# Own raw buffers and an earlier load for the modulation blocks of merge and out projection, and the neighbourhood scores in one matmul

## Chip, cores and metric

The kernel runs on one core of a Trainium2 chip. The metric is the device time of one execution in microseconds (us). TensorE (PE in the profile) multiplies, VectorE (DVE), ScalarE (ACT) and GpSimd (POOL) do elementwise work and reductions, and SyncE (SP) issues all of the loads. A DMA that SP cannot issue yet, because its buffer is still in use, holds every DMA behind it in SP's queue.

## What is computed

Two layers of a diffusion trunk. Each layer has two attention branches side by side, a gated merge of them, an output projection and a feed-forward network; 512 latent tokens and 256 context tokens go through the same weights. Cut to what matters here:

```python
for l in range(2):
    mod, mod_c = silu(c) @ w_mod[l] + b_mod[l], silu(c_ctx) @ w_mod[l] + b_mod[l]   # six vectors of 1024 each
    h, hc = modulated rms_norm of x (512 tokens) and of ctx (256 tokens), with sh1, sc1
    na_q, na_k, na_v, gq, gk, gv, ga, gb = split(h @ w_in[l]);  the same for hc
    s_win = einsum(q, k in its window) * SCALE + bias        # neighbourhood attention: 8 heads of 64
    s_ctx = einsum(q, k_ctx) * SCALE
    p = softmax(concatenate([s_win, s_ctx]))
    ya = p_win @ v_win + p_ctx @ v_ctx
    yb = grouped-query attention over all 768 keys (8 query heads, 2 key heads, rms norm and rotary)
    merged = sigmoid(ga) * (ya @ w_pa) + sigmoid(gb) * (yb @ w_pb)
    x = x + g1 * (merged @ w_o)                              # the same for ctx in layer 0
    h2 = modulated rms_norm of x, with sh2, sc2
    x = x + g2 * (silu(h2 @ w_a) * (h2 @ w_u)) @ w_ffn_out   # the same for ctx in layer 0
return rms_norm(x, final_norm)
```

`mod` is the modulation: for each token kind (latent, context) 48 blocks of 128 numbers in a layer. Blocks 0 to 15 are the shift and scale ahead of attention, 16 to 23 the gate g1, 24 to 39 the shift and scale ahead of the feed-forward network, 40 to 47 the gate g2.

## The kernel before

**Layout and arithmetic.** Activations lie feature by token: eight tiles of 128 features by 768 tokens. Every float32 product is made as three fp32r products (`steps`, L647): high part by high part, high by low, low by high. So each weight block is loaded raw into a buffer with the tag `wr` (`raw`, L626), ScalarE makes its high part `wh` (L640) and VectorE or, in most of layer 0, GpSimd makes its low part `wl` (L642). The pool of weights holds four raw buffers, three `wh` and three `wl`.

**Stages.** A layer runs through attention (`mixing`), `merge`, `out_proj` and `ffn`. In the trace layer 0's merge and output projection lie at about 430 to 620 us, layer 1's at about 1444 to 1560 us.

**Merge** (L1816). Two branches of eight steps each: the first (grouped-query branch) multiplies by `w_pb`, the second (neighbourhood branch) by `w_pa`. A step takes its gate (already there, or projected in this step by eight k-blocks of three matmuls for each of the token spans), loads and splits one weight block of 512 columns, runs the modulation blocks that `MODS` gives it, and then multiplies (`pp`) and joins on VectorE (L1866 to L1871).

**Output projection** (L1891). It runs over the tokens in two halves; in each half eight steps of 24 matmuls (`po`), with the residual added by VectorE (L1876). In the first half a step also loads and splits one block of `wo` and, where `MODS` says so, runs one modulation block.

**The modulation blocks.** `mod_one` (L727) loads one block of `wmodT`, 128 by 1024 float32 and 512 KB, into a raw buffer of the weights' pool and then reduces it on VectorE against the condition row (L722), once for each token kind: tiles `junk` (context) and `wr` (latent, in place) in the profile. `MODS` (L71) places 26 blocks (16 to 41) in layer 0, namely 7 in the first branch, 12 in the second (up to two in a step) and 7 in the output projection, and 8 blocks (40 to 47, latent only) in the second branch of layer 1. Load and reduction of a block stand next to each other in the program. The remaining blocks go beside the feed-forward network through another function, `two`.

**Order.** In merge and output projection the order on each engine, SP's queue included, is chosen by a scheduler that simulates the program with its own costs. In layer 0's attention only TensorE's order is written out. In layer 1's attention a planner (`Plan`, L309) books each instruction at a modelled cost and writes out the order of all five engines; a matmul costs it 13.3 ns and 0.4167 ns a column, at least 109 ns.

**Neighbourhood scores** (`na_pair`, L1424). A head's 512 queries go in four blocks of 128. Each block has 256 keys of its window and the 256 context keys. For each of the two halves of q (`qh`, `ql`) blocks 0 to 2 take two matmuls of 256 columns; block 3, whose window wraps around, takes three (128, 128 and 256 columns), with the keys at 384 ahead of those at 0. All of a block's matmuls of one half of q share their weights, and each is issued with a weight load of its own. The bias table `rpb` has three kinds of 256 columns, the third of them for block 3. `turn` (L1456) transposes the softmax into the key order that the values need.

Of the kernel before, what the change touches and what calls it, by code (L numbers as in the profile page):

```python
# [3 lines left out]

# [599 lines left out]
class Trunk:  # L604
# [122 lines left out]
    def mod_one(self, l, n, crow, junk):  # L727
        w = self.raw(self.d["wmodT"][l * 48 + n])
        for part in self.mod_parts(l, n, crow, junk):
            part(w)  # L730

# [692 lines left out]
    def na_pair(self, head, q, k, val, bias, out, i, pool, done=None):  # L1424
# [4 lines left out]
        def scores(s, b):  # L1429
            if b < 3:  # L1430
                parts = [(0, 256, P * b)]
            else:
                parts = [(0, P, P * b), (P, 256, 0)]
            parts.append((256, 512, S))
            for hl in range(2):
                for j, (lo, up, src) in enumerate(parts):
                    nc.tensor.matmul(
                        s[:, lo:up], q[hl][:, b * P : (b + 1) * P], k[:, src : src + up - lo],
                        start=(hl == 0 and j == 0), stop=(hl == 1 and j == len(parts) - 1), skip_group_check=True)
# [16 lines left out]
        def turn(c):  # L1456
            tp = self.ps("t", "tp")
            for b in range(2):
                for j in range(2):
                    to = 2 * j + b if c else 2 * b + j  # L1460
                    nc.tensor.transpose(
                        tp[:, to * P : (to + 1) * P], zs[b][:, (2 * c + j) * P : (2 * c + j + 1) * P], self.ident)
# [353 lines left out]
    def merge(self, l, h, ya, yd, gates, ahead, spans, pool, beside):  # L1816
# [20 lines left out]
        for br, (gname, y) in enumerate((("gb", yb), ("ga", ya))):  # L1837
# [3 lines left out]
            for j in range(KB):  # L1841
# [11 lines left out]
                if beside:  # L1853
                    for _ in range(MODS[l][br][j]):
                        beside.pop(0)()
# [35 lines left out]
    def out_proj(self, l, merged, x, nh, pool, beside):  # L1891
# [5 lines left out]
        for half in range(2):  # L1897
            a, b = half * nh, half * nh + nh
            acc = None
            for j in range(KB)[:: 1 - 2 * half]:  # L1900
# [4 lines left out]
                if half == 0 and beside and MODS[l][2][j]:  # L1905
                    beside.pop(0)()
# [385 lines left out]
    def run(self):  # L2292
# [3 lines left out]
        with (  # L2296
# [24 lines left out]
            for l in range(DEPTH):  # L2321
# [7 lines left out]
                with (  # L2329
# [12 lines left out]
                    def one(of, n):  # L2342
                        def run():
                            conditions()
                            self.mod_one(of, n, *rows)
                        return run

                    first = 40 if last else 16
                    ahead = first + sum(sum(m) for m in MODS[l])
                    beside = [one(l, n) for n in range(first, ahead)]  # L2350
                    with tc.tile_pool(name=f"m{l}", bufs=1, reuse_waits="tile") as pool_:
                        pool = _Bufs(pool_, dict(rs=2, qt=5), slots)
# [69 lines left out]
def kinds(a, b):  # L2422

    return [(f, u, s) for f, u, s in ((a, min(b, S), 0), (max(a, S), b, 1)) if f < u]

# [54 lines left out]
class Hidden:  # L2480
# [23 lines left out]
    def c21(self, ps):  # L2504
        self.t.nc.vector.tensor_tensor(self.lo, self.lo, ps, op=ALU.mult)
        return [*enumerate(self.parts(self.f), 1)]

# [78 lines left out]
def _layout(a):  # L2586
# [42 lines left out]
    d["rpb"] = np.where(inside, a["na_rpb"][:, :, dr, dc][:, :, :, None], np.float32(-BIG)).reshape(DEPTH, 8, P, 768)  # L2629
# [15 lines left out]
```

## Time and profile before

| | |
|---|---|
| median of 3 runs | 1946.68 us (1945.83 to 1948.26) |
| profiled execution | 1943.38 us, of which the span of its trace is 1940.7 us |
| TensorE busy | 1909.2 us of the span, 12300 matmuls, mean granted clock 0.998 |
| VectorE busy | 1471.7 us (76%) |
| ScalarE, GpSimd busy | 937.8 us (48%), 227.5 us (12%) |
| DMA | 210.85 MB, mean 109 GB/s |

The span runs from the first to the last instruction. A busy time is the time in which an engine has an instruction in work; matmuls overlap in part, so the pitch from one start to the next tells more of them than their own duration. "Idle before" is the time that an engine stood still ahead of an instruction, with what ended the wait behind an arrow. The granted clock is the share of TensorE's full clock that the throttle allowed.

### The profile page before, as it was taken

The numbers are of one execution on the slowest core, as the hardware profiler recorded it, in microseconds if no ns is written. First come the engines' busy times: TensorE is split into PE (matmuls) and PEld (weight loads), VectorE is DVE, ScalarE is ACT, GpSimd is POOL, SyncE is SP. The second block draws the span as 40 slices with busy tenths as digits, with TensorE's granted clock in tenths as the row PEclk, the third lists the DMA queues.
The fourth block names the chain that finished last, engine by engine and source line by source line (L and its number), as shares of the span: only waits on it lengthen the run. The fifth ranks groups of instructions, "written<-read, shape, count | busy, mean of one in ns | idle before, by whom it ended". The sixth has DMA issues, their size and how long they took to land.

```text
span 1940.7 us, 31522 instructions
## 1 busy us (share of the span) xinstructions
PE 1909.2 (98%) x12300; PEld 1764.5 (91%) x12300; DVE 1471.7 (76%) x2797; ACT 937.8 (48%) x1820; POOL 227.5 (12%) x132
## 2 busy tenths in 40 slices
PE   8999999999999999999999999999999999999998
PEld 6989999898889999999999888889988999999998
DVE  6468887769777888787868578898557587877785
ACT  4456666642226533343424345666553355544553
POOL 0432212214300000000000012132210000000000
PEclk9999999999999999999999999999999999999999
DMA  8121112235462134334443411022145532332332
GB/s 328 46 69 42 53 58 63 77 120 179 158 217 87 66 109 130 109 120 131 139 144 131 152 55 33 34 79 82 55 128 175 199 109 77 98 120 90 104 96 83
DMA packets 71670, 210.85 MB, mean 109 GB/s; under 512 B 8545, under 2 KB 10721, under 8 KB 71521
## 3 DMA queue, kind: packets, MB, share of 16 engines
q1 hardware_dynamic: 71520, 208.84, 32.9%
q8 instruction: 96, 1.57, 0.3%
q14 instruction: 54, 0.43, 0.1%
HBM read 196.75 MB, written 6.82 MB: 105 GB/s over the span
## 4 chain that ended last, share of the span: by engine, by line
PE 64%; DVE 5%; issue 1%; ACT 1%; DMA 1%; POOL 0%; SPq 0%; DVEq 0%; POOLq 0%; ACTq 0%
PE po L655 21%; PE qu L2021 14%; PE qv L2021 7%; PE pj L540 4%; PE qc L2021 3%; PE pj L655 3%; PE pf L655 3%; PE pp L655 2%; PE sc L540 2%; PE y L540 2%; PE tp L540 1%; PE pv L540 1%; ACT p L540 1%; DVE m L540 1%; DVE ptl L540 0%
## 5 line engine op out<-in xcount | busy, mean ns | idle before, releaser
L2021 PE MATMUL qu<-r,w 128*128 128x384 f32 (+1 forms) x1872 | 295.9, 310 | 0.3
L2021 PEld LDWEIGHTS qu<-r,w 128*128 128x128 f32 x1872 | 281.0, 189 | 5.0 <-DVE tt L2501 3.8
L1884 ACT ACTIVATE w<-wr 128x512 fp32r<-128x512 f32 x234 | 145.5, 625 | 107.6 <-DVE wr L2465 36.2
L655 PE MATMUL po<-ph,wh 128*128 128x512 f32 (+1 forms) x576 | 197.4, 343 | 0.0
L655 PE MATMUL po<-ph,wl 128*128 128x512 f32 (+1 forms) x576 | 196.8, 342 | 0.0
L655 PE MATMUL po<-pl,wh 128*128 128x512 f32 (+1 forms) x576 | 196.2, 341 | 0.0
L655 PE MATMUL pj<-h,wh 128*128 128x512 f32 (+1 forms) x512 | 182.1, 356 | 1.4 <-DVE ql L1256 1.1
L655 PE MATMUL pj<-h,wl 128*128 128x512 f32 (+1 forms) x512 | 176.8, 345 | 0.9 <-POOL wl L642 0.9
L655 PE MATMUL pj<-hl,wh 128*128 128x512 f32 (+1 forms) x512 | 176.6, 345 | 0.0
L1876 DVE SCALAR_TENSOR_TENSOR x<-po,G,x 128x256 f32<-128x256 f32 (+3 forms) x168 | 99.2, 596 | 100.7 <-PE po L655 99.7
L1888 DVE TENSOR_TENSOR w<-wr,w 128x512 fp32r<-128x512 f32 x234 | 159.3, 685 | 11.3 <-ACT w L1884 10.3
L640 ACT ACTIVATE wh<-wr 128x1024 fp32r<-128x1024 f32 (+1 forms) x109 | 101.3, 933 | 137.2 <-PE po L655 30.4
L2021 PE MATMUL qv<-r,w 128*128 128x384 f32 (+1 forms) x936 | 150.6, 309 | 0.3 <-ACT tt L2027 0.3
L2021 PEld LDWEIGHTS qv<-r,w 128*128 128x128 f32 x936 | 141.2, 190 | 0.5 <-ACT tt L2027 0.5
L782 POOL TENSOR_TENSOR rs<-rs,expo 128x2 f32<-128x2 f32 (+2 forms) x7 | 5.5, 784 | 1099.8 <-DVE rs L781 1099.8
L642 POOL TENSOR_TENSOR wl<-wr,wh 128x1024 fp32r<-128x1024 f32 (+1 forms) x47 | 103.5, 2205 | 229.2 <-ACT wh L640 228.9
L655 PEld LDWEIGHTS po<-ph,wl 128*128 128x128 f32 x576 | 108.2, 188 | 14.4 <-DVE wl L2192 0.4
L655 PEld LDWEIGHTS po<-pl,wh 128*128 128x128 f32 x576 | 108.5, 188 | 12.8
L655 PEld LDWEIGHTS po<-ph,wh 128*128 128x128 f32 x576 | 108.5, 188 | 12.8
L722 DVE CUSTOM_DVE_ANT_0 wr<-wr,crow 128x1024 f32<-128x1024 f32 x80 | 100.2, 1252 | 14.3 <-DMA wr<-wmodT 14.0
L655 PEld LDWEIGHTS pj<-h,wl 128*128 128x128 f32 x512 | 96.8, 189 | 13.4 <-POOL wl L642 1.3
L655 PEld LDWEIGHTS pj<-h,wh 128*128 128x128 f32 x512 | 97.0, 189 | 11.9 <-PE tp L1331 1.1
(341 smaller groups left out, 4705.7 us busy)
## 6 DMA issues: line engine op xcount, KB each, us to landing
wr<-wfi SPq DMA_DIRECT2D x88, 512.0 KB, 3.2
wr<-wmodT SPq DMA_DIRECT2D x80, 512.0 KB, 3.4
wr<-win SPq DMA_DIRECT2D x68, 512.0 KB, 3.7
wr<-wfo SPq DMA_DIRECT2D x64, 256.0 KB, 2.7
wr<-wo SPq DMA_DIRECT2D x26, 512.0 KB, 4.1
wr<-wmod SPq DMA_DIRECT2D x16, 512.0 KB, 9.9
wr<-wp SPq DMA_DIRECT2D x32, 256.0 KB, 2.9
x<-x SPq DMA_DIRECT2D x16, 384.0 KB, 7.1
```

Of the source, the lines that this page charges most:

```text
L540: ops[i]["run"](*ops[i]["args"], **ops[i]["kw"])
L640: nc.scalar.activation(hi, raw, AF.Copy)
L642: (eng or nc.gpsimd).tensor_tensor(lo, raw, hi[:].bitcast(F32), op=ALU.subtract)
L655: nc.tensor.matmul(ps[:, : b - a], u[:, c], v[k][:, a:b], start=(k == 0 and i == 0), stop=(k == nk - 1 and i == 2),)
L722: self.nc.vector.tensor_tensor_reduce(junk if s else w, w, crow[:, s], 1.0, 0.0, ALU.mult, ALU.add, self.mod[l][:, s, n : n + 1])
L782: nc.gpsimd.tensor_tensor(r[:, :nb], r[:, :nb], self.expo[:, :nb], op=ALU.pow)
L1876: self.nc.vector.scalar_tensor_tensor(x[j][:, f:u], ps[:, f - a : u - a], self.G[l][i][:, s, j : j + 1], x[j][:, f:u], op0=ALU.mult, op1=A ...
L1884: self.nc.scalar.activation(t[:, :n], src, AF.Copy)
L1888: self.nc.vector.tensor_tensor(t[:, n : 2 * n], src, t[:, :n].bitcast(F32), op=ALU.subtract)
L2021: nc.tensor.matmul(banks[bank], u[:, c], v, start=(first and k == 0 and i == 0), stop=(k == kn - 1 and i == 2), skip_group_check=True)
```

## The change

The modulation blocks of merge and output projection no longer use the weights' pool. The pool of that stage gets three raw buffers of its own (`wr=3`, 12 KB on each partition). `Loaded` counts the steps: at a step it runs the blocks that belong to it, whose loads were issued at the step before, and then issues the loads of the next step's blocks. Their number, the reductions and their places in the steps stay. The condition rows are fetched with the first load, so one step earlier.

In the scores the two matmuls of blocks 0 to 2 become one of 512 columns, whose moving operand is read in two runs of 256 (`apart`); for block 2 the two runs adjoin. Block 3 becomes one of 128 columns (keys 0 to 127) and one of 384 (keys 384 to 767). The halves of block 3's bias are swapped on the host to suit, and `turn` undoes the swap in its output place.

```diff
--- before.py
+++ after.py
@@ -1,6 +1,7 @@
 
 from collections import deque
 from contextlib import ExitStack
+from dataclasses import replace
 
 import numpy as np
 
@@ -723,11 +724,6 @@
                     junk if s else w, w, crow[:, s], 1.0, 0.0, ALU.mult, ALU.add, self.mod[l][:, s, n : n + 1])
             return run
         return [part(s) for s in ((1, 0) if l == 0 or n < 16 else (0,))]
-
-    def mod_one(self, l, n, crow, junk):
-        w = self.raw(self.d["wmodT"][l * 48 + n])
-        for part in self.mod_parts(l, n, crow, junk):
-            part(w)
 
     def mod_bias(self, l, lo, up):
         for s in range(2 if l == 0 or up <= 16 else 1):
@@ -1428,14 +1424,13 @@
 
         def scores(s, b):
             if b < 3:
-                parts = [(0, 256, P * b)]
+                parts = [(s.rearrange("p (a c) -> p a c", c=256), apart(k, P * b, S, 256))]
             else:
-                parts = [(0, P, P * b), (P, 256, 0)]
-            parts.append((256, 512, S))
+                parts = [(s[:, 0:P], k[:, 0:P]), (s[:, P:512], k[:, P * b : T])]
             for hl in range(2):
-                for j, (lo, up, src) in enumerate(parts):
+                for j, (to, keys) in enumerate(parts):
                     nc.tensor.matmul(
-                        s[:, lo:up], q[hl][:, b * P : (b + 1) * P], k[:, src : src + up - lo],
+                        to, q[hl][:, b * P : (b + 1) * P], keys,
                         start=(hl == 0 and j == 0), stop=(hl == 1 and j == len(parts) - 1), skip_group_check=True)
 
         def soft(s, b, at):
@@ -1457,7 +1452,7 @@
             tp = self.ps("t", "tp")
             for b in range(2):
                 for j in range(2):
-                    to = 2 * j + b if c else 2 * b + j
+                    to = 2 * j + b if c else 2 * b + (j if 2 * i + b < 3 else 1 - j)
                     nc.tensor.transpose(
                         tp[:, to * P : (to + 1) * P], zs[b][:, (2 * c + j) * P : (2 * c + j + 1) * P], self.ident)
             pt.append(self.split_t(tp, pool))
@@ -1850,9 +1845,7 @@
                     t = pool.tile([P, T], F32, tag="qt", name=self.name("t"))
                     drain(self.gate(l, gname, j, h, spans, lambda: t, "a"))
                 w = self.weight(d["wp"][l, 1 - br, j], 512, nc.vector if l else None)
-                if beside:
-                    for _ in range(MODS[l][br][j]):
-                        beside.pop(0)()
+                beside()
                 if br == 0:
                     mb.append(self.slot("mb"))
                 else:
@@ -1902,8 +1895,8 @@
                 if half == 0 or j < KB - 3:
                     ws[j] = self.weight(self.d["wo"][l, j], D, self.nc.vector)
                 w = ws[j]
-                if half == 0 and beside and MODS[l][2][j]:
-                    beside.pop(0)()
+                if half == 0:
+                    beside()
                 ps = self.ps("a", "po")[:, :nh]
                 self.gemm(ps, w, merged, a, b)
                 self.residual(l, 0, ps, x, j, a, b)
@@ -2339,17 +2332,17 @@
                         if not rows:
                             rows.extend(self.conditions(conds, 1 if last else 2))
 
-                    def one(of, n):
-                        def run():
-                            conditions()
-                            self.mod_one(of, n, *rows)
-                        return run
-
                     first = 40 if last else 16
                     ahead = first + sum(sum(m) for m in MODS[l])
-                    beside = [one(l, n) for n in range(first, ahead)]
                     with tc.tile_pool(name=f"m{l}", bufs=1, reuse_waits="tile") as pool_:
-                        pool = _Bufs(pool_, dict(rs=2, qt=5), slots)
+                        pool = _Bufs(pool_, dict(rs=2, qt=5, wr=3), slots)
+
+                        def one(n):
+                            conditions()
+                            w = self.raw(d["wmodT"][l * 48 + n], pool=pool)
+                            return lambda: [part(w) for part in self.mod_parts(l, n, *rows)]
+
+                        beside = Loaded([lambda n=n: one(n) for n in range(first, ahead)], sum(MODS[l], ()))
                         merged = self.merge(l, h, ya, yd, gates, others, spans, pool, beside)
                         if not last:
                             self.mod_bias(0, 16, 24)
@@ -2422,6 +2415,12 @@
 def kinds(a, b):
 
     return [(f, u, s) for f, u, s in ((a, min(b, S), 0), (max(a, S), b, 1)) if f < u]
+
+
+def apart(t, a, b, n):
+
+    near = t[:, a : a + n].unsqueeze(1).to_broadcast([P, 2, n])
+    return replace(near, ap=[near.ap[0], (b - a, 2), near.ap[2]])
 
 
 def busy(n):
@@ -2504,6 +2503,24 @@
     def c21(self, ps):
         self.t.nc.vector.tensor_tensor(self.lo, self.lo, ps, op=ALU.mult)
         return [*enumerate(self.parts(self.f), 1)]
+
+
+class Loaded:
+
+
+    def __init__(self, todo, counts):
+        self.todo, self.counts, self.ready = todo, list(counts) + [0], []
+
+    def __call__(self):
+        now = self.counts.pop(0)
+        self.fetch(now)
+        for _ in range(now):
+            self.ready.pop(0)()
+        self.fetch(self.counts[0])
+
+    def fetch(self, n):
+        while len(self.ready) < n:
+            self.ready.append(self.todo.pop(0)())
 
 
 def reach(g):
@@ -2626,7 +2643,8 @@
     constants, inside = _constants()
     d.update(constants)
 
-    d["rpb"] = np.where(inside, a["na_rpb"][:, :, dr, dc][:, :, :, None], np.float32(-BIG)).reshape(DEPTH, 8, P, 768)
+    rpb = np.where(inside, a["na_rpb"][:, :, dr, dc][:, :, :, None], np.float32(-BIG)).reshape(DEPTH, 8, P, 768)
+    d["rpb"] = np.concatenate([rpb[..., 0:512], rpb[..., 640:768], rpb[..., 512:640]], axis=-1)
     return {k: c(v) for k, v in d.items()}
```

## Prediction

> **What bounds the kernel now.** I read the page first, then the waits of single engines in layer 0's merge and output projection, since that is where the moved loads lie, then the timeline around the longest of those waits.
>
> ```profile
> PE 1909.2 (98%) x12300; PEld 1764.5 (91%) x12300; DVE 1471.7 (76%) x2797; ACT 937.8 (48%) x1820; POOL 227.5 (12%) x132
> PE po L655 <- DVE wl L642: 3.4, 2, 2.4
> PE pj L655 <- POOL wl L642: 0.9, 1, 0.9
> DVE junk L722 <- DMA wr<-wmodT: 16.0, 6, 4.2
> SPq L631 <- DVE mod L722: 66.3, 23, 5.4
> 430.00:500.00 70.00, 69.10 (x400) 60.80 (x399) 69.46 (x103) 17.11 (x27) 28.37 (x14) 1.00 0.51 167
> 500.00:560.00 60.00, 57.20 (x320) 51.45 (x318) 44.19 (x71) 18.08 (x30) 9.38 (x5) 0.97 0.54 183
> ```
>
> TensorE is busy 1909.2 of 1940.7 us, so whatever saves time must take matmul time away or close one of its few gaps; 31.5 us are all there is in gaps. The four rows of waits hold for 400 to 640 us. TensorE stands still there three times, 4.3 us in all, each time for a low part of a weight block. VectorE, which makes two of these low parts, stands still itself for 16.0 us, in six waits for a modulation block that has not landed. And SP waited 23 times, 66.3 us in all, for a reduction to free a raw buffer. The rows by stretch (length, then busy TensorE, weight loads, VectorE, ScalarE, GpSimd, then clock) say that VectorE has no room from 430 to 500 us (69.46 of 70), while from 500 to 560 us it is busy 44.19 of 60: all its waits for blocks fall into the second stretch, the one in which TensorE waits too.
>
> The gaps cost more than their length:
>
> ```profile
> 548.54 0.44 PE L655 MATMUL po<-mh,wl 128*128 128x384 f32 x1 [2.44 <-DVE wl L642]
> 560.58 0.44 PE L655 MATMUL po<-mh,wl 128*128 128x384 f32 x1 [0.94 <-DVE wl L642]
> 548.00:549.00 1.00, 0.46 (x2) 0.46 (x3) 1.00 (x2) 0.00 (x0) 0.00 (x0) 0.96 0.00 0
> 549.00:550.00 1.00, 1.00 (x4) 1.00 (x4) 1.00 (x3) 0.00 (x0) 0.00 (x0) 0.50 0.55 102
> 552.00:553.00 1.00, 1.00 (x6) 1.00 (x6) 1.00 (x3) 0.33 (x1) 0.00 (x0) 0.83 0.70 209
> 548.54 10.24 PE po L655 x48
> 662.62 6.24 PE qu L2021 x36
> ```
>
> After the gap of 2.44 us the granted clock is 0.50 from 549 to past 552 us. The chain of waits (start, length, what) shows the price: 48 matmuls of 384 columns take 10.24 us there, and 36 of the same width take 6.24 us, 0.173 us each, at full clock. 48 x 0.173 = 8.32, so the slow clock costs 1.92 us beside the 2.44. [...]
>
> Why VectorE was late, on its own timeline, with ScalarE's and SP's rows beside it:
>
> ```profile
> 524.62 1.23 DVE L722 CUSTOM_DVE_ANT_0 junk<-wr,crow 128x1024 f32<-128x1024 f32 x1 [0.62 <-DMA wr<-wmodT]
> 532.79 1.22 DVE L722 CUSTOM_DVE_ANT_0 junk<-wr,crow 128x1024 f32<-128x1024 f32 x1 [3.75 <-DMA wr<-wmodT]
> ...
> 453.35 3.99 SPq L631 DMA_DIRECT2D wr<-wmodT  x2
> 459.30 0.33 SPq L631 DMA_DIRECT2D wr<-win  x1
> ...
> 538.57 0.33 SPq L631 DMA_DIRECT2D wr<-wo  x1
> 541.92 0.33 SPq L631 DMA_DIRECT2D wr<-wmodT  x1
> 542.07 1.06 ACT L640 ACTIVATE wh<-wr 128x1024 fp32r<-128x1024 f32 x1 [2.50 <-issue]
> 546.12 1.22 DVE L722 CUSTOM_DVE_ANT_0 junk<-wr,crow 128x1024 f32<-128x1024 f32 x1 [4.22 <-DMA wr<-wmodT]
> 547.27 1.22 DVE L642 TENSOR_TENSOR wl<-wr,wh 128x1024 fp32r<-128x1024 f32 x1
> 555.20 1.22 DVE L722 CUSTOM_DVE_ANT_0 junk<-wr,crow 128x1024 f32<-128x1024 f32 x1 [1.97 <-DMA wr<-wmodT]
> 559.31 2.35 DVE L642 TENSOR_TENSOR wl<-wr,wh 128x1024 fp32r<-128x1024 f32 x2
> ```
>
> The high part that the stalled matmul needs was done at 543.13 (542.07 + 1.06). Its low part came at 547.27, since a reduction stood ahead of it on VectorE, waiting until 546.12 for a block that SP could issue only at 541.92. So low parts wait behind reductions, reductions behind loads, and loads behind a ring of four buffers which weights and modulation blocks share.
>
> **The change part by part.** *Loads in buffers of their own, one step ahead.* Nothing is added or removed: 26 loads in layer 0 and 8 in layer 1, and as many reductions. What moves is each load's issue, ahead by about a step, past the weight loads of that step on SP's queue.
>
> ```profile
> L722 DVE CUSTOM_DVE_ANT_0 wr<-wr,crow 128x1024 f32<-128x1024 f32 x80 | 100.2, 1252 | 14.3 <-DMA wr<-wmodT 14.0
> wr<-wmodT SPq DMA_DIRECT2D x80, 512.0 KB, 3.4
> x<-x SPq DMA_DIRECT2D x8, 384.0 KB, 7.7
> wr<-wmodT SPq DMA_DIRECT2D x3, 512.0 KB, 6.4
> DVE wr L722 <- DMA wr<-wmodT: 14.0, 8, 3.8
> ```
>
> A step of the output projection is 24 x 0.173 = 4.16 us of matmuls. A load lands 3.4 us after its issue (second row, whole kernel), so one issued a step ahead is there in time, and the 10.6 us that VectorE idles between 524 and 556 us (0.62 + 3.75 + 4.22 + 1.97 in the rows above) fall away. They are more than twice the 4.1 us (543.13 to 547.27) by which the low part of the first gap was late. So I take that gap and its slow clock as gone: 2.44 + 1.92 = 4.36 us. The gap of 0.90 at 467 us waits for GpSimd's low part of a gate block, whose load SP issued at 459.30, behind two modulation blocks that took it from 453.35 to 457.34 for want of buffers; with a ring free of them it can be issued earlier, so this is gone too (bounds: 0 to 0.90). The gap of 0.94 falls together with the eight loads of x: between 545 and 565 us (the third and fourth row) these take 7.7 us to land and the blocks of the modulation 6.4, longer than a step. I leave this gap standing (bounds: 0 to 0.94 gained). Together 4.36 + 0.90 = 5.26 us, with bounds from 0 to 6.20.
>
> A new wait is possible in steps with two blocks: two wait in buffers, two more are to be loaded, and there are three buffers. The fourth load stands at the head of SP's queue until a reduction ends, and the next weight block stands behind it. Such waits exist already (SP's 66.3 us above), so I price this at nothing more in the forecast, and as a rival below. Layer 1 gains nothing: VectorE waits there too (last row, 1440 to 1560 us, 14.0 us), but no wait of TensorE is listed in that stretch, so its matmuls are the cover; only the number of matmuls decides there.
>
> *Scores.* Matmul pitches from the chain of waits and from TensorE's timeline:
>
> ```profile
> 1363.43 8.64 PE pv L540 x72
> 1395.60 8.20 PE pj L540 x36
> 288.20 0.50 PE L1437 MATMUL sc<-k,qh 128*128 128x128 f32 x3
> ...
> 288.88 0.40 PE L655 MATMUL pj<-h,wh 128*128 128x512 f32 x1
> 1311.77 0.95 PE sc L540 x8
> 1317.25 1.16 PE sc L540 x10
> ```
>
> 256 columns take 8.64 / 72 = 0.120 us, 512 take 8.20 / 36 = 0.228, so two become one at a gain of 0.012. Block 3's three take 0.34 (two groups of three in 0.68 us), of which 0.120 for the 256 columns and 0.110 for each of the 128. Afterwards 0.110 + 0.173 (384 columns) = 0.283, a gain of 0.057. A head has three plain blocks and one wrapped one, each for two halves of q: 2 x (3 x 0.012 + 0.057) = 0.186 us. It fits the last two rows: blocks 0 and 1 now 0.95, then 4 x 0.228 = 0.91; blocks 2 and 3 now 1.16, then 1.02. Eight heads and two layers: 3.0 us, with 128 matmuls fewer. In both attention stages TensorE sets the pace, except here:
>
> ```profile
> 1408.16 3.31 DMA bias<-rpb
> 1419.15 0.44 PE L540 MATMUL tp<-ident_sb,z 128*128 128x128 f32 x2 [1.22 <-DVE z L540]
> PE pj L540 <- ACT kg L540: 2.3, 1, 2.3
> PE sc L540 <- ACT p L540: 1.5, 3, 0.7
> ```
>
> From 1403 to 1419 us the chain runs through the load of a bias and VectorE, and what TensorE saves inside it only makes the 1.22 us longer. I take off 0.3 us for it and count 2.7.
>
> No row shows a moving operand that is read in two runs. Below: it streams as a plain 512 (0.228). Above: it goes at the pace of the 128-column matmuls, 4 x 0.110 = 0.44, which over the 64 of them that are really split (blocks 0 and 1, two halves, eight heads, two layers) would cost 64 x (0.44 - 0.228) = 13.6 us. I take the lower end, as the same columns are read in the same order as before and only the address jumps once. Swapped bias and transposes: as many instructions of the same size, nothing.
>
> Sum: 5.26 + 2.7 = 8.0 us. From the profiled execution's 1943.38 that gives 1935.4; it lies 3.3 us under the median of the runs, so I put the gain on the median: 1946.68 - 8.0 = **1938.7 us**.
>
> **The rivals.** *Scores alone:* VectorE stays late, because it is full until 500 us and the loads of x fill the DMA queues afterwards; the gap stays near 2.4 us, its slow clock with it. For it speaks VectorE's 69.46 of 70 us, against it that all 16.0 us of waiting come after 500. It gives 1946.68 - 2.7 = 1944.0.
>
> *The planner takes it back:* layer 1's attention is booked anew with cheaper scores, so the order of all five engines there can change. Its gaps (the 2.3 and 1.5 above among them) can grow; if as much again is lost as these two rows hold, 3.8 us, the result is 1938.7 + 3.8 = 1942.5. They can shrink as well: 1934.9.
>
> *Slower:* the fourth load of a two-block step blocks SP's queue. Five steps of the second branch have two blocks. Each of them needs its gate's weights, and where these are late by over 2.4 us, the gap draws the slow clock behind it: 4.36 us a time, as above. Two such gaps would eat the gain (8.7 against 8.0); with three it is 1946.68 - 8.0 + 13.1 = 1951.8. Against it: SP waits for these reductions today for up to 5.4 us, and only 0.9 us of it reaches TensorE. It decides from the point at which a weight block is issued some 5 us later than now.
>
> [...]
>
> **How the numbers follow.** Forecast 0.60, its own range 1937.5 (all gaps and the 3.0 us of scores: 9.2) to 1941.5 (a gap of 1.2 us left without a slow clock, 2.0 us of scores: 5.2). Scores alone 0.15. Planner against it 0.09, for it 0.04. Slow clock stays 0.04. Blocked queue, slower, 0.08. About 0.2%, 3.9 us, is what a measurement of this kernel can tell from no change, so faster means below 1942.8. That holds for nearly all of the forecast, the slow clock's case, the favourable planner and half of the unfavourable one: 0.70. Scores alone and the rest of these lie within 0.2%: 0.22. Slower: 0.08. The range runs from 1934.5 (the favourable planner) to 1945.5 (scores alone with the spread of the runs); the blocked queue and the edges beyond stay out.
>
> **What would show it.** 12172 matmuls, with scores of 512 and 384 columns at pitches of 0.228 and 0.173; a pitch near 0.44 would mean that two runs are expensive. Between 500 and 560 us VectorE's waits for modulation blocks fall from 16.0 to under 4 us, and the clock stays at 1.00. SP issues a block a step or more ahead of its reduction. It would be wrong if TensorE shows a gap behind a late weight block in the second branch, or if VectorE, without its waits, still gives low parts late.

## The result and the profile after

The changed kernel takes 1949.71 us (median of 22 runs, 1946.65 to 1952.3) and the kernel before, beside it, 1945.23 us (22 runs). The ratio is 1.002 with a 95% interval of 1.0013 to 1.0027: slower by 4 us, 2.5 to 5.3. The forecast was 1938.7 us, 0.4% faster, and its range ended at 1945.5. The profiled execution of after took 1952.05 us, its span 1950.3.

The page of after, and then its waits for 400 to 640 us, those of TensorE first, then the longest of VectorE's and of SP's (engine, line, what it waited for: us in total, times, longest):

```profile
PE 1911.9 (98%) x12172; PEld 1763.7 (90%) x12172; DVE 1475.4 (76%) x2797; ACT 937.0 (48%) x1820; POOL 229.4 (12%) x132
```

```profile
PE pj L656 <- DVE t L1861: 6.4, 3, 2.8
...
DVE x L1869 <- PE po L656: 21.4, 14, 3.6
...
SPq L632 <- DVE mod L723: 72.3, 22, 5.0
```

128 matmuls are gone, as the diff says. The two kinds of wait that the prediction wanted closed are gone as well: no wait of TensorE for a low part of a weight, none of VectorE for a block of the modulation. In their place stands one that before does not have: three times, 6.4 us in all, TensorE waits with a gate projection (`pj`) for `t`, VectorE's evacuation of an earlier product. SP waits for reductions about as long as before (72.3 us, 66.3 before), and nothing of TensorE waits for a late weight.

The lengths of the stages, from the starts of their first matmuls (rounded to 0.1 us, so a length can be off by as much), in us of one profiled execution each; the fourth row runs from the end of the last `qu`, a product of layer 0's feed-forward network, to layer 1's first score. "Paced" is an experiment further down:

```
stage                          before   after  scores  loads   paced
                                               alone   alone   loads
attention, layer 0              334.3   337.2   337.5   334.6   334.5
merge, layer 0                  118.1   125.6   119.3   125.6   117.0
output projection, layer 0       73.5    67.9    71.0    67.9    67.9
last qu to first score          104.6   106.1   106.1   106.1   106.1
attention, layer 1              263.1   265.3   265.6   266.5   264.3
span                           1940.7  1950.3  1947.3  1948.6  1938.1
```

The output projection is 5.6 us shorter; the two gaps of before and the slow clock behind the first make 5.30 of it (2.44 + 0.94 + 1.92), of which the forecast had counted 4.36. Merge is 7.5 us longer and attention of layer 0 is 2.9 us longer. Attention of layer 1 is 2.2 us longer: near its end TensorE waits 1.07 and 1.98 us for VectorE ahead of two transposes, where before has one wait of 1.22, and the clock is 0.60 and 0.55 in the two stretches of 2 us from 1426. The attention stages come up with the scores further down; why merge is longer shows on VectorE. Reductions of the modulation alone (line 722, 723 in the others), by stretch: start and end, length, busy time of VectorE with the number of instructions, then clock and DMA. A reduction is two instructions and a block of layer 0 two reductions, so four instructions are a block. First before (merge, then output projection), then after:

```profile
423.80:541.90 118.10, 63.80 (x88) 1.00 0.49 161
541.90:615.50 73.60, 9.82 (x16) 0.98 0.50 173
```

```profile
427.20:552.80 125.60, 74.28 (x104) 0.99 0.49 165
552.80:620.80 68.00, 0.00 (x0) 1.00 0.42 146
```

Before ran 22 blocks inside merge and 4 in the output projection. After ran all 26 inside merge: none is left for the stage in which `MODS` has 7. Of one step of the second branch, on VectorE's timeline of after (start, length, instruction):

```profile
506.94 0.68 DVE L1861 SCALAR_TENSOR_TENSOR t<-t,pp 128x512 f32<-128x512 f32 x1
507.54 1.21 DVE L723 CUSTOM_DVE_ANT_0 wr<-wr,crow 128x1024 f32<-128x1024 f32 x1
...
515.14 2.30 DVE L723 CUSTOM_DVE_ANT_0 junk<-wr,crow 128x1024 f32<-128x1024 f32 x1
...
517.37 2.61 DVE L1864 TENSOR_TENSOR ml<-t,mh 128x256 fp32r<-128x256 f32 x1
519.90 1.21 DVE L723 CUSTOM_DVE_ANT_0 wr<-wr,crow 128x1024 f32<-128x1024 f32 x1
...
521.05 1.22 DVE L723 CUSTOM_DVE_ANT_0 junk<-wr,crow 128x1024 f32<-128x1024 f32 x1
...
522.20 1.01 DVE L1861 SCALAR_TENSOR_TENSOR t<-t,pp 128x512 f32<-128x512 f32 x2
```

From the first `t` of one step (506.94) to that of the next (522.20) VectorE does eight reductions, four blocks; the step has at most two. The last two stand directly ahead of the second `t` and take 2.30 us (519.90 to 522.20). TensorE, on its own timeline, waits 2.50 us for just that, and twice more:

```profile
523.02 0.47 PE L656 MATMUL pj<-h,wh 128*128 128x512 f32 x1 [2.50 <-DVE t L1861]
...
538.61 0.48 PE L656 MATMUL pj<-h,wh 128*128 128x512 f32 x1 [2.83 <-DVE t L1861]
538.92 0.60 PE L656 MATMUL pj<-hl,wh 128*128 128x512 f32 x1
...
542.30 0.43 PE L656 MATMUL pj<-h,wh 128*128 128x512 f32 x1
```

After the third gap eight matmuls of 512 columns take 3.38 us (538.92 to 542.30), 0.42 each instead of the 0.23 further on: the slow clock again, some 1.5 us. So the gap and its slow clock were not removed. They moved from the output projection into merge, with a new releaser.

### The profile page after: what moved, and what is told of

Same layout as the page of the kernel before. It is cut to its first block, busy times and chain, and to the rows that moved or that the text cites. A ratio compares the mean times of both kernels' runs of the same rounds, so it can differ in the third digit from the quotient of the medians.

```text
span 1950.3 us, 31235 instructions
## 1 busy us (share of the span) xinstructions
PE 1911.9 (98%) x12172; PEld 1763.7 (90%) x12172; DVE 1475.4 (76%) x2797; ACT 937.0 (48%) x1820; POOL 229.4 (12%) x132
## 4 chain that ended last, share of the span: by engine, by line
PE 84%; DVE 11%; ACT 2%; issue 2%; DMA 1%; POOL 0%; SPq 0%; DVEq 0%; POOLq 0%; ACTq 0%
PE po L656 21%; PE qu L2014 14%; PE pj L656 11%; PE qv L2014 7%; PE pj L541 4%; PE qc L2014 3%; PE pf L656 3%; PE pp L656 3%; DVE junk L723 2%; PE y L541 2%; DVE wr L723 2%; PE sc L541 2%; PE pv L1218 2%; PE tp L541 1%; PE pj L946 1%
## 5 line engine op out<-in xcount | busy, mean ns | idle before, releaser
L656 PEld LDWEIGHTS pj<-hl,wh 128*128 128x128 f32 x512 | 98.2, 192 | 10.1
```

Source lines behind the costliest of these rows:

```text
L656: nc.tensor.matmul(ps[:, : b - a], u[:, c], v[k][:, a:b], start=(k == 0 and i == 0), stop=(k == nk - 1 and i == 2),)
```

## The experiments

The ratio of each run is against the kernel before on the same chip. The theories on the loads: **A**, a ring of their own unties the blocks from the weights; the scheduler then queues reductions as early as the ring allows, ahead of the evacuations that TensorE needs. **B**, it is the load one step ahead that does harm. **D**, VectorE beside GpSimd is too full there in any order. On the scores: the joined matmuls cost or gain by themselves, or through the order on other engines (rivals with other letters are spelled out in the expectations).

**The two halves of the change, each alone.** The scores with the loads of before, then the loads with the scores of before.

The first takes back all that the diff does to the modulation blocks, the second all that it does to `scores`, `turn` and the bias:

```diff
-                beside()
+                if beside:
+                    for _ in range(MODS[l][br][j]):
+                        beside.pop(0)()
```

```diff
-                parts = [(s.rearrange("p (a c) -> p a c", c=256), apart(k, P * b, S, 256))]
+                parts = [(0, 256, P * b)]
             else:
-                parts = [(s[:, 0:P], k[:, 0:P]), (s[:, P:512], k[:, P * b : T])]
+                parts = [(0, P, P * b), (P, 256, 0)]
+            parts.append((256, 512, S))
```

> The scores' part of the change alone, with the loads of the modulation blocks as before. Theory A (the own buffers of the modulation blocks are what costs): TensorE spends some 2 us less on scores, the merge keeps its length of before (118 us from the first matmul of the first branch to the first of the output projection), and the time is 1 to 3 us under before. Rival C (the scores cost, by a changed order in the attention stages): the attention stages get longer, as in the changed kernel (by 2.9 us in layer 0 and 2.2 us in layer 1), and the time is 2 to 5 us above before.

> The loads' part alone, with the scores as before. Theory A: all 26 reductions of layer 0 end before the output projection begins; TensorE waits in the merge's second branch for VectorE to free a bank (6 to 7 us in all, with the slow clock behind it), the merge takes some 126 us in place of 118 and the output projection some 68 us in place of 73.5; the time is 1 to 4 us above before. Rival C: the merge and output projection together no longer than before, and the time is the same as before within 2 us.

Scores alone: 1.0006 (0.9997 to 1.0015), no gain where 2.7 us were forecast. Loads alone: 1.0017 (1.0006 to 1.0027), 3 us over instead of 5 under. Each half misses by itself, and the table above shows that in these traces each makes its own stage longer.

**Own ring without the step ahead, and the step ahead without the ring.** In both the scores are those of before. Without the first fetch each load is issued at its own step; without a pool of their own the blocks go back to the weights' buffers.

```diff
-        self.fetch(self.counts[0])
```

```diff
-                        pool = _Bufs(pool_, dict(rs=2, qt=5, wr=3), slots)
+                        pool = _Bufs(pool_, dict(rs=2, qt=5), slots)
...
-                            w = self.raw(d["wmodT"][l * 48 + n], pool=pool)
+                            w = self.raw(d["wmodT"][l * 48 + n])
```

> Own three buffers for the modulation blocks, but each block loaded in its own step, not one ahead; scores as before. Theory A (own buffers untie the blocks from the steps): the same reductions ahead of time as with the whole loads' part, all 26 before the output projection, waits of TensorE for VectorE in the second branch, and 1 to 4 us above before. Rival B (the load one step ahead is what brings the reductions forward): the reductions stay spread as before, 22 of them in the merge, and the time is that of before within 2 us.

> Loads one step ahead, but from the four raw buffers that the weights use too; scores as before. Theory A: the shared ring keeps the blocks in step with the weights; some 24 reductions end in the merge, no wait of TensorE for VectorE's evacuation in the second branch, and a time within 3 us of before. Rival B: the reductions come ahead as in the changed kernel, with its waits in the second branch, 1 to 4 us above before.

Ring only: 1.002 (1.0007 to 1.0032), the loss of the whole of the loads' part, with the same merge (125.6), all 26 blocks in it, and the same row of waits:

```profile
PE pj L656 <- DVE t L1862: 6.4, 3, 2.8
```

B falls. Ahead only: 1.0026 (1.0014 to 1.0038), worse than expected, and for another reason. Its waits of TensorE in 400 to 640 us:

```profile
PE pj L656 <- ACT wh L641: 2.9, 1, 2.9
PE pp L656 <- POOL wl L643: 1.3, 2, 0.7
PE pj L656 <- POOL wl L643: 0.8, 1, 0.8
PE pp L656 <- ACT wh L641: 0.7, 1, 0.7
...
```

No `t` is among them, and two to three of the 26 blocks stay in the output projection. Blocks that wait a step ahead in shared buffers hold these from the weights: SP issues the gate block that the longest wait needs at 466.44, where before issued it at 459.30. So TensorE waits for parts of weights, 5.7 us in all. The early load does need the ring.

**Smaller rings.** If A holds, a ring of one leaves no room to run ahead, and a ring of two half as much.

```diff
-                        pool = _Bufs(pool_, dict(rs=2, qt=5, wr=3), slots)
+                        pool = _Bufs(pool_, dict(rs=2, qt=5, wr=1), slots)
```

> The loads' part with one own buffer in place of three, in the scheduler's free order; scores as before. Theory A (it is the blocks running free that costs, not buffers of their own): with one buffer a block can follow only after the reduction and the load of the one before, some 6 us, so that the reductions spread by themselves; some 20 in the merge, no or little waiting for VectorE's evacuation there, the merge at 117 to 120 us. What it then costs or gains in the output projection, where six blocks are left and each reduction waits for its load, is open: 68 to 74 us. The time is 1 to 8 us under before. Rival (own buffers cost by themselves): merge over 122 us.

> The same with two own buffers. Theory A: two buffers let load and reduction overlap, all 26 reductions end before the output projection as with three, the waits in the second branch are there (3 to 7 us), the merge takes 121 to 126 us and the time is between before and the loads' part alone: 0 to 3.5 us above before.

The order went as A says: merge 118.7 us with one buffer, 123.3 with two, 125.6 with three. The time did not: one buffer took 1.008 (1.0065 to 1.0095), 16 us over, a clear miss. Its waits of 400 to 640 us, then those of the ring of two:

```profile
PE po L656 <- DVE wl L643: 6.4, 1, 6.4
...
DVE junk L723 <- DMA wr<-wmodT: 45.8, 24, 3.1
```

```profile
PE pj L656 <- DVE t L1862: 4.1, 2, 3.0
...
DVE junk L723 <- DMA wr<-wmodT: 3.4, 4, 1.5
```

With one buffer only 16 of the 26 blocks lie in merge (20 were expected), VectorE waits for nearly each block, 24 times and 45.8 us, and everything behind it on its queue waits too: what held up the kernel before, made worse. Two buffers lie between, at 1.0012 (1.0001 to 1.0022). A ring's size sets the landing of the loads and the pace of the reductions at once, and none of the three sizes sets both right.

**The ring of three with the pace given back.** A step's reductions are queued on VectorE behind the join (`ml`, `mb` or the residual) of the step before, or of the one before that; in the second run `[-1]` and `1` become `[-2]` and `2`. Loads and ring are those of after, the scores those of before.

```diff
-        for _ in range(now):
-            self.ready.pop(0)()
+        with trunk.tc.issue_after(self.behind[-1]) if len(self.behind) >= 1 else nullcontext():
+            for _ in range(now):
+                self.ready.pop(0)()
...
                         nc.vector.tensor_tensor(lo[:, a:b], t[:, a:b], hi[:, a:b].bitcast(F32), op=ALU.subtract)
+                beside.behind.append(joined.ins)
```

> The loads' part with the scores as before, and each step's reductions queued on VectorE behind the join of the step before it, so that no reduction of a later step can stand ahead of an evacuation. Theory A (reductions ahead of time in VectorE's queue are what costs): no wait of TensorE for VectorE's evacuation in the second branch, the merge back at about 118 us, the output projection at 68 to 70 us, and the time 2 to 6 us under before, or 4 to 8 us under the loads' part alone. Rival D (VectorE has too much to do in the merge in any order, since GpSimd slows it): the merge stays over 122 us, or the output projection goes back to 73 us, and nothing is gained on before.

> As the run before, but the reductions queue behind the join of two steps before. Theory A: as there, with a merge of 118 to 120 us; the reductions may come a step earlier, which frees the output projection of one more of them. Rival D: merge over 122 us again.

0.9959 (0.9945 to 0.9972) and 0.9957 (0.9945 to 0.9969): some 8 us under, with medians of 1939.58 and 1939.89 beside 1947.86 for before. The windows of the second, all engines (length, then busy TensorE, weight loads, VectorE, ScalarE, GpSimd, clock), merge and output projection, and below them its reductions alone:

```profile
424.60:541.60 117.00, 117.00 (x675) 103.45 (x674) 105.78 (x152) 31.24 (x53) 43.52 (x20) 1.00 0.48 163
541.60:609.50 67.90, 67.90 (x398) 67.90 (x397) 54.78 (x97) 30.00 (x46) 0.85 (x1) 1.00 0.48 169
```

```profile
424.60:541.60 117.00, 62.84 (x80) 1.00 0.48 163
541.60:609.50 67.90, 14.47 (x24) 1.00 0.48 169
```

TensorE stands still nowhere in 185 us, at full clock. 20 blocks lie in merge and 6 in the output projection. GpSimd is busy for 43.52 of merge's 117 us and VectorE for 105.78, and nothing is late: D falls. A is shown from both sides: free reductions lose 7.5 us in merge, held ones take 1.1 us off it, with the same buffers and loads.

**The scores, layer by layer.** One layer joined, the other as before. For layer 1 once with the planner booking the old cost (the first two lines), so that TensorE's order stays, and once with its own booking; for layer 0 the order of the other engines is the scheduler's.

```diff
+            if op != "transpose" and (len(aps[0].ap) > 2 or n == 384):
+                return 2 * FIX + n * 0.4167e-3 if n == 512 else PASS + FIX + 256 * 0.4167e-3
...
-            if b < 3:
-                parts = [(0, 256, P * b)]
+            if self.layer not in JOINED:
+                parts = [(0, 256, P * b)] if b < 3 else [(0, P, P * b), (P, 256, 0)]
...
+            elif b < 3:
+                parts = [(s.rearrange("p (a c) -> p a c", c=256), apart(k, P * b, S, 256))]
```

> The scores in one matmul in layer 1 alone, with the planner booking them at the cost of the matmuls that they replace, so that it writes out nearly the order of before; layer 0 and the loads as before. Theory E (the score matmuls save their 1.0 us a layer, and the changed order gives it back): the attention of layer 1 takes 262 to 263 us, without the wait of 2.0 us for the softmax at its end, and the time is 0 to 2 us under before. Rival F (the joined matmuls cost by themselves): layer 1's attention again 2 us longer, the time 1 to 3 us above before.

> The kernel before with the scores joined in layer 1 alone, at the planner's own cost, so that it plans the order of all five engines anew. If the new plan is what costs (gaps near 1424 us in the whole change, 1.98 and 1.07 us for the transposes), 1 to 3 us over the kernel before; the run with the old bookings and the old order came out even. If layer 1 takes no part, within 1 us.

> The scores in one matmul in layer 0 alone, layer 1 and the loads as before. Theory E: layer 0's attention has the waits of TensorE for VectorE's low parts of q of the changed kernel (1.6 to 1.9 us and 1.75 us), which cost more than the 1.0 us saved; the time is 0 to 3 us above before. Rival G (the order of layer 1 alone costs): layer 0's attention no longer than 334 us, time 1 us under before.

Layer 1 makes no difference: 0.9999 (0.9988 to 1.0009) in the old order, 0.9995 (0.9985 to 1.0005) in the new one; the gain of up to 2 us did not come. Layer 0 costs: 1.0012 (1.0002 to 1.0022). Yet the matmuls are cheaper. The windows of the tile `sc` in the two attention stages, before and then after (busy TensorE is the first number behind the length):

```profile
89.50:423.80 334.30, 55.00 (x336) 45.31 (x336) 60.67 (x80) 51.48 (x128) 1.00 0.21 65
...
1186.20:1449.30 263.10, 45.83 (x272) 37.26 (x272) 51.04 (x64) 32.84 (x64) 1.00 0.22 69
```

```profile
90.00:427.20 337.20, 53.76 (x272) 40.60 (x272) 60.66 (x80) 51.48 (x128) 0.99 0.22 68
...
1192.60:1458.00 265.40, 44.85 (x208) 32.35 (x208) 50.95 (x64) 32.84 (x64) 0.99 0.22 74
```

1.24 us less in layer 0 and 0.98 in layer 1, for 128 matmuls fewer. Waits for VectorE eat it in layer 0. TensorE's waits in layer 0's attention and the first steps of merge (97 to 437 us), before, then layer 0 joined:

```profile
PE pj L655 <- DVE ql L1256: 1.1, 2, 0.9
PE tp L1461 <- DVE z L1275: 0.9, 1, 0.9
...
PE pv L1222 <- DVE ql L1256: 0.5, 1, 0.5
```

```profile
PE pj L657 <- DVE ql L1258: 2.7, 2, 1.7
PE pv L1224 <- DVE ql L1258: 1.7, 1, 1.7
PE tp L1465 <- DVE z L1277: 1.2, 1, 1.2
```

TensorE's order is written out and the same but for the joined matmuls. On ScalarE and VectorE the scheduler chose anew: it put the exponentials of the context items (`p<-sc,m`) ahead of a high part of q. Two rows of before, then three with layer 0 joined:

```profile
364.93 0.54 ACT L1255 ACTIVATE qh<-pj 64x448 fp32r<-64x448 f32 x1 [0.78 <-DVE ql L1256]
...
365.53 0.48 ACT L1368 ACTIVATE p<-sc,m 128x256 f32<-128x256 f32 x1
```

```profile
367.43 0.48 ACT L1370 ACTIVATE p<-sc,m 128x256 f32<-128x256 f32 x1 [1.26 <-DVE m L1361]
...
368.48 0.54 ACT L1257 ACTIVATE qh<-pj 64x448 fp32r<-64x448 f32 x1
...
373.02 0.39 PE L657 MATMUL pj<-h,wh 128*128 128x256 f32 x1 [1.75 <-DVE ql L1258]
```

**Layer 0 joined, with that order held.** The exponentials of the context items are queued on ScalarE behind the high part of q (`up`), the reciprocals of their sums on VectorE behind the low part (`down`). The edges, of the class `NoSync`, order one engine's own queue.

```diff
+                    if v and l == 0 and a == 0 and f:
+                        told = self.told
+                        for exp, soft in self.context[told:]:
+                            for ins, of in ((exp, up), (soft, down)):
+                                if ins is not None:
+                                    self.tc.add_manual_dep(ins, of.ins.name, mybir.DependencyInfo(
+                                        mybir.DependencyClass.NoSync, mybir.DependencyReason.DATA), reason="order")
```

> The kernel before with the scores joined in layer 0 alone, as in the run with layer 0 alone, but the exponentials of the context items and their sums are held behind the high and low parts of q, by order edges without a wait of their own, so that ScalarE and VectorE take these in about the order of the kernel before. Theory (the loss of that run is the changed order on ScalarE and VectorE): the new wait of TensorE of 1.75 us for a low part of q near 373 us is gone, the one of 1.65 near 314 us is back at about 0.5, layer 0's attention takes 335 us or less (334.3 before, 337.6 in the run with layer 0 alone) and the time is 0 to 2 us under the kernel before. Rival (VectorE bounds these stretches, and what TensorE saves only becomes waiting): attention of layer 0 still 336 to 338 us, the waits turn up at other places, and the time is 1 to 3 us over.

1.0001 (0.9993 to 1.001), and attention of layer 0 takes 334.2 us, as before (334.3), instead of 337.6. Its waits in the same stretch:

```profile
PE pj L659 <- DVE ql L1264: 1.3, 2, 0.9
PE tp L1479 <- DVE z L1290: 1.1, 1, 1.1
PE pv L1230 <- DVE ql L1264: 1.1, 1, 1.1
```

Both theories hold a part. The order was the loss: the wait of 1.75 us is 0.35, and 3.4 us of the stage come back. Not all of these are the order's, though. With layer 0 joined in free order the clock is halved at 170 us, where it is full in before and in the held order:

```profile
170.00:172.00 2.00, 2.00 (x8) 1.81 (x8) 1.56 (x5) 1.95 (x4) 2.00 (x1) 0.50 0.58 180
```

The same matmuls lie 0.35 us apart in these two traces at 168 us and 1.93 at 174, so 1.6 of the 3.4 us are this slow clock, which two runs that leave layer 0's scores alone show as well (the ring of one and a paced run below). Some 1.8 us are left for the order; the timed runs, 1.0012 against 1.0001, say about 2. And these waits are still 1.0 us longer than before (3.5 against 2.5 in the three rows), the wait near 314 us at 1.06 and not at 0.5, and 1.24 us were saved: in these places TensorE waits for VectorE, and a faster TensorE only waits longer. In after, with both layers joined, 1.5 of the 2.9 us of this stage are slow clock too (0.50 from 371.7 to 375.1 us), there right behind the wait of 1.75 us.

**Pacing with the scores joined.** All three have the pacing of the second paced run. The first is the whole change with it; the second has the scores joined in layer 1 alone, in the old order; the third in layer 0 alone, in the held order. The edits are those shown above; besides the way in which the order is held, the second and third differ in

```diff
-JOINED = (1,)
+JOINED = (0,)
```

> The whole change, scores too, with the reductions queued behind the join of two steps before. Theory A with the scores' own result (1.2 us above before): 6 to 8 us under before. If the scores' cost and the loads' cost were one and the same thing, it would be 8 us or more under before.

> The loads' part with that order, and the scores in one matmul in layer 1 alone, booked at their old cost. As each alone gave 8.0 us and nothing: 7.5 to 9.5 us under before, the same as the loads' part with its order alone within what can be told apart.

> The loads in their own ring with the reductions held behind the join of the step before the last (8.2 us under the kernel before when run alone), plus the scores of layer 0 joined in the held order. Theory: merge and output projection of layer 0 stay at 117.0 and 67.9 us, and the joined scores take nothing back: 8 to 10 us under the kernel before. Rival: they cost as in the run of the whole change with that pacing: 3 to 6 us under.

0.9985 (0.9975 to 0.9995), 0.9979 (0.9969 to 0.9988) and 0.9975 (0.9964 to 0.9987): 2.9, 4.1 and 4.9 us under. The first two missed their expectation, the third came out as its rival said, and none reaches the 8 us of the paced loads alone, though each has merge and output projection of layer 0 at 117 and 67.9 us. For the first, layer 0's attention (336.0 us) tells a part. For the other two this stays open: an interval of 0.9964 to 0.9987 touches that of 0.9945 to 0.9969, and a single trace does not settle a difference of 3 us, for this reason. In layer 1's attention of the third, where nothing was changed, stands a wait that before does not have. Below it are the rows that make it, and VectorE's row of before for the same work:

```profile
PE tp L543 <- DVE p L543: 2.4, 1, 2.4
```

```profile
1302.52 2.34 POOL L543 TENSOR_TENSOR wl<-wr,wh 128x1024 fp32r<-128x1024 f32 x1 [0.35 <-ACT wh L543]
...
1302.69 2.83 DVE L543 TENSOR_SCALAR p<-p,rc 128x768 f32<-128x768 f32 x1
```

```profile
1305.26 0.62 DVE L540 TENSOR_SCALAR p<-p,rc 128x768 f32<-128x768 f32 x1
```

The wait stands in the traces of ten of the fifteen experiments, whether layer 1 was touched or not, the first paced run among them and the second not. In all ten GpSimd begins a low part some 0.2 us ahead of VectorE's `p`, which then takes 2.8 us. In the other seven traces, before and after among them, VectorE comes first, GpSimd begins its low part some 0.75 us later (1306.02 in before), and `p` takes 0.62. So it depends on which of the two engines comes first there; what decides that was not followed. The slow clock behind the wait is as irregular: five of the ten have it. Holding the order in layer 1 as well, and more runs of these three on one chip, were not tried.

The paced loads with the scores of before are the best version: 8 us under the kernel before, 12 under the change.

## Why the prediction was wrong

**The reading of before was right.** Loads were late, reductions waited for them, low parts stood behind reductions: with buffers of their own, VectorE's 16.0 us of waits went to nothing, and the output projection lost 5.6 us. Even the gap of 0.94, which was left standing, closed. Where the reductions kept their places (paced), the gain was 8 us, beside 5.26 forecast for the loads; 6.8 of it show in the trace's two stages (191.7 to 184.9), a little over the forecast's upper bound of 6.20.

**The step that failed**: "Nothing is added or removed: 26 loads in layer 0 and 8 in layer 1, and as many reductions. What moves is each load's issue, ahead by about a step". The reductions moved too: seven blocks left the stage where `MODS` has them, where before three had (the section on the change, too, says that they stay). The working took their places from `MODS`, that is from the program's text, while the order in these stages comes from a scheduler. What had kept the reductions near their steps was the shared ring, the very thing removed: a block could not be loaded before the weights ahead of it had left a buffer, and a reduction cannot run before its load. The two runs that part ring and early load bear this out: 26 of 26 blocks in merge with the own ring alone, 23 to 24 with the shared one. The row that gave the warning was quoted: VectorE busy for 69.46 of 70 us from 430 to 500. It was read as a reason why VectorE might stay late, not as a queue in which each reduction that comes early makes something else late. In merge of after that something is `t`.

**The slower rival had another mechanism.** It feared for SP's queue and a late weight. SP's waits for reductions hardly grew (66.3 to 72.3 us), and no weight was late with the ring of three. The sign was covered at 0.08, the cause by none of the rivals.

**The scores were right in kind and off in size and place.** Reading in two runs costs nothing that shows: starts of 512-column scores in after lie 0.23 us apart (the prediction took 0.228), and the upper bound of 13.6 us falls. The saving in busy time is 2.2 us and not 3.0. But "In both attention stages TensorE sets the pace, except here" failed in layer 0: it held neither at 314 nor at 373 us, where TensorE waits for low parts of q, and with the scheduler's answer to cheaper matmuls layer 0 joined alone came out 2.3 us over before (0.4 to 4.3) instead of under it. The step excepted only the place that it had a row for. The rival of the planner in layer 1 does not show in the time: joined there alone, with a new plan, it is the same within 0.15%. The gap of 1.22 us that the prediction quotes did grow, though, to 0.65 and 1.45 us in that run and to 1.07 and 1.98 in after.

**The slow clock.** 1.92 us behind the gap were counted rightly for the trace of before, but as a price that the gap's length sets, from 2.4 us on: an estimate from that one gap. The last section shows that it is not so: the clock stays full behind 2.50 us and halves behind 2.35. Nor did it stay slow without its gap (0.04 in the forecast): in the output projection of after it is 1.00. (The lower end of the range, 1934.5, is called the favourable planner's, whose sum gives 1934.9; nothing hangs on it.)

## What to carry to other kernels

A shared buffer ring is also a brake: before giving a stream its own buffers, ask what keeps its consumers in their place afterwards, and where a scheduler orders the engines, write that place down (here an order edge to the join of a step before: with the loads alone 0.9957 with it, 1.0017 without). Check in the new trace how many of the moved instructions each stage holds, not only whether their waits are gone. And count a saving on the busiest engine only between its waits: where the next thing on its path waits for another engine, the saving becomes waiting (in layer 0, order held, 1.24 us saved and 1.0 us of longer waits).

## What the hardware showed beside this

**The clock does not go by the length of a gap alone.** In one and the same trace of after, TensorE's clock stays full behind the gap of 2.50 us that ends at 523.0, and halves behind that of 2.83 us at 538.6:

```profile
524.00:526.00 2.00, 2.00 (x10) 1.64 (x9) 2.00 (x5) 0.00 (x0) 0.00 (x0) 1.00 0.28 61
...
539.00:540.00 1.00, 1.00 (x4) 0.81 (x3) 1.00 (x3) 0.00 (x0) 0.00 (x0) 0.50 0.00 0
```

The same gap of 2.35 us ahead of a projection of layer 1, at 1174.9 in before and at 1179.8 in after, is followed by a full clock in the one and a halved one in the other:

```profile
1176.00:1178.00 2.00, 2.00 (x20) 2.00 (x19) 2.00 (x1) 0.07 (x1) 2.00 (x1) 1.00 0.86 233
```

```profile
1181.00:1183.00 2.00, 2.00 (x11) 2.00 (x11) 2.00 (x1) 0.00 (x0) 2.00 (x1) 0.50 0.86 249
```

That alone is the 1.5 us between 104.6 and 106.1 us in the table's fourth row. No edit goes with it: this gap is 2.34 or 2.35 us in all seventeen traces, and the clock halves behind it in ten of them and stays full in seven, before and the first paced run among the seven, the second paced run among the ten. It halves behind a gap of 0.58 us too (at 170 us with layer 0 joined, above), where it stays full behind the same gap in before. A halved stretch lasts some 3.4 us (538.9 to 542.4 in after) or twice that (471.4 to 478.2 with the early load alone) in the stages told of here. What decides it is not shown. Single executions of one kernel differ by several us as well, the 22 runs of before from 1940.5 to 1953.08: the two spans differ by 9.6 us where the timed runs differ by 4.

**Some of what runs on VectorE beside GpSimd takes longer.** In after, GpSimd makes two low parts from 514.52 to 519.70 (5.18 us). In that time a reduction takes 2.30 us instead of 1.21, and a `ml` of 256 columns 2.61 us (rows of the step above) where the shortest of the same kind takes 0.42. These stretched instructions stand ahead of the `t` of 522.20 as well, and add to what the early reductions cost there. In layer 1's attention the same thing makes or unmakes the whole wait of 2.4 us shown above: VectorE's `p` takes 2.8 us beside a low part that GpSimd began first, and 0.62 where GpSimd had not begun. Not all is stretched: the `mb` of 512 columns at 457.74, all of it beside a low part that GpSimd makes from 457.25 to 458.95, takes 0.68, as the shortest of its kind.
